# A two-layer hybrid decoder trunk: the third and the last right factor of each seven-product block summed by accumulating loads

## The chip, the cores and the metric

The kernel runs on one core of one Trainium2 chip. The metric is the device time of one execution in microseconds. The engines are called PE (TensorE: matmuls and their weight loads), DVE (VectorE), ACT (ScalarE), POOL (GpSimd) and SP (SyncE, which here issues loads). DRAM-to-SBUF loads run on 16 DMA engines that all issuing queues share.

## The reference

256 tokens of width 1024 go through two layers, each of an FFN, a mixer (a state-space part, pooling and attention) and a second FFN, with norms around each. The change touches the FFNs alone:

```python
def _swiglu(h, wg, wu, wd):
    return (jax.nn.silu(h @ wg) * (h @ wu)) @ wd

for l in range(DEPTH):                      # DEPTH = 2
    f = _swiglu(_rmsnorm(h, ff1_norm_pre[l]), ff1_w_gate[l], ff1_w_up[l], ff1_w_down[l])
    h = h + 0.5 * _rmsnorm(f, ff1_norm_post[l])
    ...                                     # the mixer
    f = _swiglu(_rmsnorm(h, ff2_norm_pre[l]), ff2_w_gate[l], ff2_w_up[l], ff2_w_down[l])
    h = h + 0.5 * _rmsnorm(f, ff2_norm_post[l])
```

`wg` and `wu` are 1024 x 2816, `wd` is 2816 x 1024, all float32.

## The kernel before, in words

**Precision.** A weight of 1 MB (128 partitions x 2048 floats, 8 KB each) is loaded into a place called `raw`. It is then split into a rounded part `hi` (a copy on ACT, line 98) and the rest `lo` (raw minus hi, on DVE, line 99), each in two steps of 128x1024. Activations are split in the same way (lines 199 and 200). Every product is then three passes of matmuls: hi by hi, hi by lo, lo by hi.

**The FFN.** The 2816 columns are 11 units of 256. Units 0 and 1 are done plainly (`ffn_first`); 4, 7 and 10 as pairs of a gate and an up product (`ffn_pair`, lines 285 to 287); 2 and 3, 5 and 6, 8 and 9 as blocks of seven products in place of eight (`ffn_quad`, line 416). For a block let g1, g2 be the upper and lower half (512 rows) of its gate columns and u1, u2 those of its up columns. The right factors are

| name | value | before |
|---|---|---|
| g1, g2, u2 | as loaded | as loaded |
| T1 | g1 + u1 | DVE add, into u1's place |
| T2 | T1 + u2 | DVE add, into u1's place |
| T3 | u1 + u2 = T2 - g1 | DVE subtraction, into g1's place |
| T4 | T2 + g2 | DVE add, into u1's place |

Each add or subtraction stands on line 97, in two steps of 128x1024, ahead of the split of its sum. There are 12 blocks (three in each of four FFNs), so 48 sums and 96 steps. The left factors are sums of quarters of the activations, made once per FFN (S1 to S4). Behind each block or pair the down projections of the units before it follow (`mm_rows`, line 322): the hidden activations are turned by PE (line 391), copied and split by ACT and DVE (199, 200) into buffers of the tag "t", and multiplied with two token tiles in turn. In the first two blocks of an FFN a down projection stands between two of the products; in the last (units 8 and 9, `late`) none stands before u2's.

**What sets the order.** `plan_ffn` lists loads (`W.unit`) and splits (`W.job`). There are four places for raw weights and five for split ones; `pump` loads as soon as a place is free and splits as soon as fewer than five splits are held. A place is given back when the last job that reads it has been split (`free`). `product` and `mm_rows` take splits in the order in which PE is to use them. The framework then orders the instructions of each engine once, when the program is built; on the chip each engine takes its queue strictly in order, and one that waits holds all that is behind it. Loads are issued by SP; POOL has only the 28 reciprocal square roots of the norms (line 210) and five settings of constants at the start.

In the places below, `hiN` and `loN` are the splits of the N-th job, `rawN` is the place of the N-th load, `t` and `wk` are temporaries in SBUF and PSUM.

Of the kernel before, what the change touches and what calls it, by code (L numbers as in the profile page):

```python
# [13 lines left out]
AF = mybir.ActivationFunctionType  # L14
ALU = mybir.AluOpType
AX = mybir.AxisListType

P = 128
# [10 lines left out]
UNIT = 2048  # L29
# [18 lines left out]
class Weights:  # L48
# [9 lines left out]
        self.units.append((src, cols))  # L58
        return len(self.units) - 1

    def job(self, unit, sum_of=None, free=(), pieces=2):


        self.jobs.append((unit, sum_of, free, pieces))
        return len(self.jobs) - 1

    def plan(self, src, cols=UNIT, pieces=2):
# [17 lines left out]

    def split_next(self):
        i, nc = self.split, self.nc
        u, sum_of, free, pieces = self.jobs[i]
        cols, raw = self.units[u][1], self.raw[u]
        hi = self.splitp.tile([P, KD * QDT], F32R, tag="hi", name=f"hi{i}")  # L90
        lo = self.splitp.tile([P, KD * QDT], F32R, tag="lo", name=f"lo{i}")
        step = cols // pieces
        for c in range(0, cols, step):
            s = slice(c, c + step)
            if sum_of:
                x, op, y = sum_of
                nc.vector.tensor_tensor(raw[:, s], self.raw[x][:, s], self.raw[y][:, s], op=op)  # L97
            nc.scalar.activation(hi[:, s], raw[:, s], AF.Copy)  # L98
            nc.vector.tensor_tensor(lo[:, s], raw[:, s], hi[:, s].bitcast(F32), op=ALU.subtract)  # L99
        for v in free:  # L100
            del self.raw[v]
            self.live -= 1
        self.parts[i] = (hi, lo)
        self.split += 1
        self.held += 1
# [25 lines left out]
def hybrid_trunk_kernel(ctx: ExitStack, tc: tile.TileContext, a, out: bass.AP):  # L131
    nc = tc.nc
# [3 lines left out]
    tmp = ctx.enter_context(tc.tile_pool(name="tmp", bufs=1))  # L136
# [3 lines left out]
    ids = iter(range(10**6))  # L140

    def buf(dtype=F32, n=512, tag="t"):
        return tmp.tile([P, n], dtype, tag=tag, name=f"{tag}{next(ids)}", bufs={"t": 22, "n": 8}[tag])

    def tiny(n):
        return small.tile([P, n], F32, tag=f"s{n}", name=f"s{next(ids)}", bufs=2 if n > 64 else 12)
# [1 line left out]
    def bank(tag="wk"):  # L148
        return psum.tile([P, 512], F32, tag=tag, name=f"{tag}{next(ids)}")
# [176 lines left out]
    def plan_ffn(l, n):  # L326


        p = {}

        def down(i):
            p["d", i] = W.plan(a[f"ff{n}_d"][l, i])

        def pair(i):
            for k in "gu":
                p[k, i] = W.plan(a[f"ff{n}_{k}"][l, PAIRS.index(i)])

        for i in range(2):
            for k in range(2):
                p["f", i, k] = W.plan(a[f"ff{n}_f"][l, 2 * i + k], pieces=4)  # L340
        before = list(FIRST)
        for i in range(2, NU):
            if i in PAIRS:
                pair(i)
                for b in before:
                    down(b)
                before = [i]
            elif i in QUADS:
                src = a[f"ff{n}_q"][l, QUADS.index(i)]
                g1, u1, u2 = (W.unit(src[k]) for k in (0, 1, 3))  # L350
                p["T1", i] = W.job(u1, (g1, ALU.add, u1))
                p["g1", i] = W.job(g1)
                p["T2", i] = W.job(u1, (u1, ALU.add, u2))
                p["T3", i] = W.job(g1, (u1, ALU.subtract, g1), free=(g1,))
                late = i == QUADS[-1]
                if not late:
                    down(before[0])
                g2 = W.unit(src[2])
                p["g2", i] = W.job(g2)
                for b in before[1:]:  # L360
                    down(b)
                p["T4", i] = W.job(u1, (u1, ALU.add, g2), free=(u1, g2))
                p["u2", i] = W.job(u2, free=(u2,))
                if late:
                    down(before[0])
                before = [i, i + 1]
        for b in before:
            down(b)
        return p
# [40 lines left out]
    def product(ps, left, job, first):  # L410

        hi, lo = (w[:, :UNIT].rearrange("p (k n) -> p k n", k=4) for w in W.get(job))
        parts = [(k, i) for k in range(4) for i in range(2)] + [(k, 2) for k in range(4)]
        for n, (k, i) in enumerate(parts):
            x, w = ((left[0], hi), (left[0], lo), (left[1], hi))[i]
            nc.tensor.matmul(ps, x[:, k, :], w[:, k, :], start=first and n == 0, stop=n == len(parts) - 1,  # L416
                             skip_group_check=not first)
        W.done(job)

    def ffn_quad(i, p, left, turn, downs):  # L420


        late = i == QUADS[-1]
        turn(0)
        pc = bank()
        product(pc, left["S1"], p["T1", i], True)
        h1 = buf()
        nc.scalar.activation(h1, pc, AF.Copy)
        pa = bank()
        product(pa, left["X11"], p["g1", i], True)  # L430
        w2 = buf()
        nc.scalar.activation(w2, pa, AF.Copy)
        turn(1)
        W.pump()
        pb = bank()
# [1 line left out]
        nc.vector.tensor_tensor(w2, pb, w2, op=ALU.add)  # L437
        nc.vector.tensor_tensor(pc, pc, w2, op=ALU.subtract)  # L438
        W.pump()
        pd = bank()  # L440
        product(pd, left["S3"], p["T3", i], True)
        nc.vector.tensor_tensor(pd, pd, w2, op=ALU.add)
        nc.vector.tensor_tensor(h1, h1, pd, op=ALU.subtract)
        W.pump()
        if not late:
            downs[0]()
        product(pa, left["X12"], p["g2", i], False)
        h0 = buf()
        nc.scalar.activation(h0, pa, AF.Silu)
# [609 lines left out]
```

## Time and profile before

| | |
|---|---|
| runs | median 964.05 us of 3 (962.85 to 965.3) |
| profiled execution | 964.58 us, of which the span is 962.5 us |
| PE, DVE, ACT busy | 940.0, 814.6, 584.3 us |
| line 97 (sums of factors) | 96 steps, 113.7 us on DVE |
| line 99 (lo), 128x1024 | 344 steps, 403.6 us on DVE |
| loaded | 176 MB; DMA engines 49.6% of their time |
| PE's granted clock | 0.991 on average |

Busy times are unions of an engine's instructions. Matmuls are pipelined and their ends are modelled, so their rate is read from the starts of consecutive ones: 12 matmuls with 512 columns take 2.72 us undisturbed. A place where PE loses time shows as more time between two such starts, and only partly as idle time. In a timeline, a number in brackets is the engine's idle time before the row and what ended it.

### The profile page before, as it was taken

How to read it: one execution, taken by the hardware profiler on the slowest of the kernel's cores; microseconds unless marked ns; L12 is line 12 of the kernel's file. 1: busy time of each engine (PE TensorE's matmuls, PEld its weight loads, DVE VectorE, ACT ScalarE, POOL GpSimd, SP SyncE). 2: the span in 40 equal slices, each digit the busy share in tenths (PEclk: the TensorE clock that was granted, in tenths of full speed). 3: DMA queues.
4: the chain of work that ended last, by engine and by line, in shares of the span. 5: the costliest groups of instructions: out<-in, count | busy, mean ns of one | idle time of the engine just before them, and what ended most of it. 6: DMA issues, size and time to landing. Idle time of an engine off the chain costs nothing.

```text
span 962.5 us, 13043 instructions
## 1 busy us (share of the span) xinstructions
PE 940.0 (98%) x5064; PEld 800.9 (83%) x5064; DVE 814.6 (85%) x1088; ACT 584.3 (61%) x923; POOL 19.7 (2%) x33
## 2 busy tenths in 40 slices
PE   8999999999999999999999999999999999999997
PEld 5679898988988779898977888898888877979895
DVE  5997899688797989899598989986878798889982
ACT  7665566467656565566466656666584565656651
POOL 0000000010001000000000000000000100000000
PEclk9989999999999999999999999999999999999999
DMA  7464365755243355466642727293733242927241
GB/s 295 186 251 186 144 250 206 277 182 212 88 144 116 109 210 228 158 236 232 249 175 81 295 109 284 95 362 135 268 124 131 88 154 88 345 92 300 93 177 44
DMA packets 26706, 178.03 MB, mean 185 GB/s; under 512 B 2962, under 2 KB 3346, under 8 KB 6292
## 3 DMA queue, kind: packets, MB, share of 16 engines
q1 hardware_dynamic: 26644, 177.19, 49.6%
q8 instruction: 40, 0.66, 0.3%
q14 instruction: 22, 0.18, 0.1%
HBM read 176.13 MB, written 1.05 MB: 184 GB/s over the span
## 4 chain that ended last, share of the span: by engine, by line
PE 77%; DVE 13%; ACT 5%; issue 2%; DMA 2%; POOL 1%; SPq 0%; DVEq 0%; POOLq 0%; ACTq 0%
PE acc L322 25%; PE wk L416 21%; PE wk L286 6%; PE wk L285 6%; PE wk L287 6%; DVE lo L99 6%; PE wk L307 5%; DVE raw L97 3%; ACT hi L98 2%; ACT n L216 1%; PE wk L391 1%; DMA raw<-in_ff_q 1%; DVE n L200 1%; POOL s L210 1%; PE wk L852 1%
## 5 line engine op out<-in xcount | busy, mean ns | idle before, releaser
L98 ACT ACTIVATE hi<-raw 128x1024 fp32r<-128x1024 f32 (+2 forms) x440 | 399.3, 958 | 179.6 <-DVE raw L97 57.6
L99 DVE TENSOR_TENSOR lo<-raw,hi 128x1024 fp32r<-128x1024 f32 (+2 forms) x440 | 466.1, 1100 | 15.7 <-ACT hi L98 14.7
L322 PE MATMUL acc<-hi,t 128*128 128x512 f32 x832 | 238.4, 395 | 3.3 <-DVE t L200 1.4
L322 PEld LDWEIGHTS acc<-hi,t 128*128 128x128 f32 x832 | 154.4, 188 | 38.5 <-ACT t L199 4.5
L285 PE MATMUL wk<-xT,hi 128*128 128x256 f32 x544 | 156.1, 287 | 0.0
L286 PE MATMUL wk<-xT,hi 128*128 128x256 f32 x544 | 154.8, 285 | 0.0
L287 PE MATMUL wk<-xT,lo 128*128 128x256 f32 x544 | 154.7, 284 | 0.0
L322 PE MATMUL acc<-lo,t 128*128 128x512 f32 x416 | 133.0, 391 | 4.1 <-DVE lo L99 4.1
L307 PE MATMUL wk<-hi,xT 128*128 128x512 f32 x384 | 124.4, 399 | 3.8 <-ACT xT L199 2.2
L416 PE MATMUL wk<-hi,n 128*128 128x512 f32 x384 | 126.6, 394 | 0.0
L97 DVE TENSOR_TENSOR raw<-raw,raw 128x1024 f32<-128x1024 f32 x96 | 113.7, 1216 | 2.5 <-DMA raw<-in_ff_q 2.5
L286 PEld LDWEIGHTS wk<-xT,hi 128*128 128x128 f32 x544 | 105.1, 193 | 0.7
L285 PEld LDWEIGHTS wk<-xT,hi 128*128 128x128 f32 x544 | 105.1, 193 | 0.6
L287 PEld LDWEIGHTS wk<-xT,lo 128*128 128x128 f32 x544 | 104.9, 193 | 0.1
L322 PEld LDWEIGHTS acc<-lo,t 128*128 128x128 f32 x416 | 77.7, 188 | 21.9 <-DVE lo L99 5.9
L416 PE MATMUL wk<-hi,xT 128*128 128x512 f32 x288 | 94.6, 389 | 0.0
L307 PEld LDWEIGHTS wk<-hi,xT 128*128 128x128 f32 x384 | 72.9, 191 | 21.4 <-ACT xT L199 3.3
L416 PEld LDWEIGHTS wk<-hi,n 128*128 128x128 f32 x384 | 73.1, 190 | 15.7 <-DVE wk L438 0.2
L307 PE MATMUL wk<-lo,xT 128*128 128x512 f32 x192 | 76.2, 398 | 0.6 <-DVE lo L99 0.6
L416 PE MATMUL wk<-lo,n 128*128 128x512 f32 x192 | 75.8, 395 | 0.0
L416 PEld LDWEIGHTS wk<-hi,xT 128*128 128x128 f32 x288 | 54.1, 188 | 11.6
L199 ACT ACTIVATE t<-wk 128x256 fp32r<-128x256 f32 x72 | 26.9, 378 | 54.7 <-PE wk L391 34.6
(182 smaller groups left out, 840.1 us busy)
## 6 DMA issues: line engine op xcount, KB each, us to landing
raw<-in_ff_q SPq DMA_DIRECT2D x48, 1024.0 KB, 7.1
raw<-in_ff_d SPq DMA_DIRECT2D x44, 1024.0 KB, 7.0
raw<-in_ff_f SPq DMA_DIRECT2D x15, 1024.0 KB, 5.1
raw<-in_ff_g SPq DMA_DIRECT2D x12, 1024.0 KB, 5.3
raw<-in_ff_u SPq DMA_DIRECT2D x12, 1024.0 KB, 4.9
raw<-in_w_in SPq DMA_DIRECT2D x10, 1024.0 KB, 5.6
raw<-in_w_kvz SPq DMA_DIRECT2D x8, 1024.0 KB, 7.0
raw<-in_w_out SPq DMA_DIRECT2D x8, 1024.0 KB, 4.9
```

Source lines behind the costliest of these rows:

```text
L97: nc.vector.tensor_tensor(raw[:, s], self.raw[x][:, s], self.raw[y][:, s], op=op)
L98: nc.scalar.activation(hi[:, s], raw[:, s], AF.Copy)
L99: nc.vector.tensor_tensor(lo[:, s], raw[:, s], hi[:, s].bitcast(F32), op=ALU.subtract)
L199: nc.scalar.activation(hi, src_f32, AF.Copy)
L200: nc.vector.tensor_tensor(lo, src_f32, hi.bitcast(F32), op=ALU.subtract)
L210: nc.gpsimd.tensor_tensor(r, v, halfexp, op=ALU.pow)
L285: nc.tensor.matmul(ps, hi[:, k, s], x[0][:, k, :], start=k == 0, stop=False)
L286: nc.tensor.matmul(ps, hi[:, k, s], x[1][:, k, :], start=False, stop=False)
L287: nc.tensor.matmul(ps, lo[:, k, s], x[0][:, k, :], start=False, stop=k == KD - 1)
L307: nc.tensor.matmul(ps, y[:, k, :], w[:, k, :], start=h == 0 and n == 0, stop=h == 1 and n == len(parts) - 1)
L322: nc.tensor.matmul(acc[b], x[:, j, s], w[:, j, b * 512 : (b + 1) * 512], start=first and j == 0 and i == 0, stop=last and j == 1 and i == 2)
L416: nc.tensor.matmul(ps, x[:, k, :], w[:, k, :], start=first and n == 0, stop=n == len(parts) - 1, skip_group_check=not first)
```

## The change

The block's sums are made differently. T1 is summed by DVE into g1's place (after g1 itself has been split), T2 too. u2 is loaded a second time, onto u1 in u1's place, by a load that adds to what is there: this makes T3. g2 is loaded a second time onto T2 in g1's place: this makes T4. Both loads are issued by POOL, T3's when T1 has been summed and u1 is read no more, T4's when T2 has been split. The first product is g1's, then T1's; T3's split comes after the next down projection's, and that down projection ahead of T3's product (not in the last block). The temporaries of tag "t" are 20 instead of 22, and the space for descriptors of POOL's loads is 4096 instead of 1024 bytes.

```diff
-    def job(self, unit, sum_of=None, free=(), pieces=2):
-        self.jobs.append((unit, sum_of, free, pieces))
+    def job(self, unit, sum_of=None, free=(), pieces=2, then=None):
+        self.jobs.append((unit, sum_of, free, pieces, then))
...
             nc.scalar.activation(hi[:, s], raw[:, s], AF.Copy)
             nc.vector.tensor_tensor(lo[:, s], raw[:, s], hi[:, s].bitcast(F32), op=ALU.subtract)
+        if then:
+            nc.gpsimd.dma_start(self.raw[then[0]][:, :UNIT], then[1], accum_op=ALU.add)
...
-        return tmp.tile([P, n], dtype, tag=tag, name=f"{tag}{next(ids)}", bufs={"t": 22, "n": 8}[tag])
+        return tmp.tile([P, n], dtype, tag=tag, name=f"{tag}{next(ids)}", bufs={"t": 20, "n": 8}[tag])
...
                 g1, u1, u2 = (W.unit(src[k]) for k in (0, 1, 3))
-                p["T1", i] = W.job(u1, (g1, ALU.add, u1))
                 p["g1", i] = W.job(g1)
-                p["T2", i] = W.job(u1, (u1, ALU.add, u2))
-                p["T3", i] = W.job(g1, (u1, ALU.subtract, g1), free=(g1,))
+                p["T1", i] = W.job(g1, (g1, ALU.add, u1), then=(u1, src[3]))
+                p["T2", i] = W.job(g1, (g1, ALU.add, u2), then=(g1, src[2]))
                 late = i == QUADS[-1]
                 if not late:
                     down(before[0])
+                p["T3", i] = W.job(u1, free=(u1,))
                 g2 = W.unit(src[2])
-                p["g2", i] = W.job(g2)
+                p["g2", i] = W.job(g2, free=(g2,))
                 for b in before[1:]:
                     down(b)
-                p["T4", i] = W.job(u1, (u1, ALU.add, g2), free=(u1, g2))
+                p["T4", i] = W.job(g1, free=(g1,))
                 p["u2", i] = W.job(u2, free=(u2,))
...
         turn(0)
+        pa = bank()
+        product(pa, left["X11"], p["g1", i], True)
+        w2 = buf()
+        nc.scalar.activation(w2, pa, AF.Copy)
         pc = bank()
         product(pc, left["S1"], p["T1", i], True)
         h1 = buf()
         nc.scalar.activation(h1, pc, AF.Copy)
-        pa = bank()
-        product(pa, left["X11"], p["g1", i], True)
-        w2 = buf()
-        nc.scalar.activation(w2, pa, AF.Copy)
         turn(1)
...
+        if not late:
+            downs[0]()
         pd = bank()
         product(pd, left["S3"], p["T3", i], True)
         nc.vector.tensor_tensor(pd, pd, w2, op=ALU.add)
         nc.vector.tensor_tensor(h1, h1, pd, op=ALU.subtract)
         W.pump()
-        if not late:
-            downs[0]()
         product(pa, left["X12"], p["g2", i], False)
...
-    nc = _bacc.Bacc("TRN2", target_bir_lowering=False, num_devices=1, dynamic_dma_scratch_size=1024)
+    nc = _bacc.Bacc("TRN2", target_bir_lowering=False, num_devices=1, dynamic_dma_scratch_size=4096)
```

The lines shift: 97 becomes 98 (sums), 98 becomes 99 (hi), 99 becomes 100 (lo), 199 and 200 become 202 and 203, 322 becomes 325, 375 becomes 378, 391 becomes 394, 416 becomes 419, 210 becomes 213; the accumulating load is line 102.

**First place: DVE, the first FFN's first block.** `raw4` is g1, `raw5` u1, `raw6` u2, `raw7` the next down projection. Before:

```order
L97 TENSOR_TENSOR raw5_223<-raw4_211,raw5_223 128x1024 x2
L375 TENSOR_TENSOR t41_309<-wk39_258,t40_307 128x512
L99 TENSOR_TENSOR lo4_250<-raw5_223,hi4_249 128x1024
L99 TENSOR_TENSOR lo5_366<-raw4_211,hi5_365 128x1024
L99 TENSOR_TENSOR lo4_250<-raw5_223,hi4_249 128x1024
L99 TENSOR_TENSOR lo5_366<-raw4_211,hi5_365 128x1024
L375 TENSOR_TENSOR t45_363<-wk43_312,t44_361 128x512
L97 TENSOR_TENSOR raw5_223<-raw5_223,raw6_235 128x1024 x2
L97 TENSOR_TENSOR raw4_211<-raw5_223,raw4_211 128x1024
L99 TENSOR_TENSOR lo6_372<-raw5_223,hi6_371 128x1024 x2
L99 TENSOR_TENSOR lo7_380<-raw4_211,hi7_379 128x1024
L97 TENSOR_TENSOR raw4_211<-raw5_223,raw4_211 128x1024
```

And with the change:

```order
L100 TENSOR_TENSOR lo4_250<-raw4_211,hi4_249 128x1024 x2
L378 TENSOR_TENSOR t41_307<-wk39_256,t40_305 128x512
L98 TENSOR_TENSOR raw4_211<-raw4_211,raw5_223 128x1024 x2
L100 TENSOR_TENSOR lo5_364<-raw4_211,hi5_363 128x1024 x2
L378 TENSOR_TENSOR t45_361<-wk43_310,t44_359 128x512
L98 TENSOR_TENSOR raw4_211<-raw4_211,raw6_235 128x1024 x2
L203 TENSOR_TENSOR t47_398<-wk50_401,t46_397 128x2x128
L100 TENSOR_TENSOR lo6_373<-raw4_211,hi6_372 128x1024
L100 TENSOR_TENSOR lo7_382<-raw7_247,hi7_381 128x1024
L100 TENSOR_TENSOR lo6_373<-raw4_211,hi6_372 128x1024
L100 TENSOR_TENSOR lo7_382<-raw7_247,hi7_381 128x1024
L100 TENSOR_TENSOR lo8_390<-raw5_223,hi8_389 128x1024 x2
```

g1's split now stands first and T1's sum behind it; T3's two steps on `raw4` are gone, the down projection's split (`raw7`) stands ahead of T3's (`lo8` from `raw5`), which was ahead of it.

**Second place: ACT, the second FFN's first block.** `hi62` is T2 (before), `hi63` T3 and `hi64` the down projection before; with the change `hi62` is T2, `hi63` the down projection and `hi64` T3. `t331` and `t333` are the hi parts of the turned hidden activations of units 0 and 1; `wk335` holds the first token tile's, `wk340` the second's. Before:

```order
L199 ACTIVATE t331_3085<-wk335_3089 128x2x128
L98 ACTIVATE hi63_3067<-raw51_2620 128x1024
L98 ACTIVATE hi64_3077<-raw54_2898 128x1024
L98 ACTIVATE hi63_3067<-raw51_2620 128x1024
L98 ACTIVATE hi64_3077<-raw54_2898 128x1024
L199 ACTIVATE t333_3087<-wk335_3089 128x2x128
L199 ACTIVATE t331_3085<-wk340_3128 128x2x128
```

And with the change:

```order
L99 ACTIVATE hi62_3054<-raw51_2614 128x1024
L99 ACTIVATE hi63_3063<-raw54_2892 128x1024
L99 ACTIVATE hi62_3054<-raw51_2614 128x1024
L99 ACTIVATE hi63_3063<-raw54_2892 128x1024
L99 ACTIVATE hi64_3071<-raw52_2868 128x1024 x2
L202 ACTIVATE t331_3079<-wk335_3083 128x2x128
L202 ACTIVATE t331_3079<-wk340_3122 128x2x128
L202 ACTIVATE t333_3081<-wk335_3083 128x2x128
```

The first tile's turn stood ahead of T3's hi; now both tiles' turns stand behind T3's, which comes from the place that the accumulating load fills. In the first FFN's first block the first tile's turn is still ahead of T3's hi, and the second tile's is behind it.

**Third place: DVE, the first FFN's last block**, with the change (`raw23` is g1, `raw24` u1, `raw25` u2, `raw26` g2):

```order
L98 TENSOR_TENSOR raw23_957<-raw23_957,raw25_1002 128x1024 x2
L378 TENSOR_TENSOR t91_1167<-wk87_1050,t90_1165 128x512
L100 TENSOR_TENSOR lo31_1183<-raw23_957,hi31_1182 128x1024
L203 TENSOR_TENSOR t83_1046<-wk89_1156,t82_1045 128x2x128
L203 TENSOR_TENSOR t93_1170<-t91_1167,t92_1169 128x512
L203 TENSOR_TENSOR t85_1048<-wk89_1156,t84_1047 128x2x128
L100 TENSOR_TENSOR lo31_1183<-raw23_957,hi31_1182 128x1024
L100 TENSOR_TENSOR lo32_1216<-raw24_980,hi32_1215 128x1024 x2
L100 TENSOR_TENSOR lo33_1248<-raw26_1024,hi33_1247 128x1024 x2
L100 TENSOR_TENSOR lo34_1286<-raw23_957,hi34_1285 128x1024 x2
```

Between T2's split (`lo31`) and T4's (`lo34`, from the place that the second accumulating load fills) only T3's and g2's splits stand; no sum is left behind T2's. On PE this block's order is g1, T1, T2, T3, g2, nine matmuls of u2, T4.

More of the change, by code (lines that the diff above doesn't have):

```diff
@@ L87, in split_next @@
         i, nc = self.split, self.nc
-        u, sum_of, free, pieces = self.jobs[i]
+        u, sum_of, free, pieces, then = self.jobs[i]
         cols, raw = self.units[u][1], self.raw[u]
```

## The prediction

> **What bounds the kernel now.** I read the page's first part, then a table of stretches of 20 us, then, where TensorE (PE) loses time, the timelines of PE, VectorE (DVE) and ScalarE (ACT) and the chain of waits.
>
> ```profile
> span 962.5 us, 13043 instructions
> PE 940.0 (98%) x5064; PEld 800.9 (83%) x5064; DVE 814.6 (85%) x1088; ACT 584.3 (61%) x923; POOL 19.7 (2%) x33
> ```
>
> ```profile
> 40.00:60.00 20.00, 16.46 (x59) 12.19 (x58) 17.82 (x21) 12.14 (x16) 0.00 (x0) 0.83 0.29 108
> ...
> 320.00:340.00 20.00, 18.67 (x84) 14.54 (x82) 20.00 (x25) 12.21 (x18) 0.00 (x0) 1.00 0.11 44
> ...
> 360.00:380.00 20.00, 20.00 (x139) 18.68 (x138) 18.43 (x21) 12.96 (x17) 0.00 (x0) 1.00 0.76 293
> ...
> 500.00:520.00 20.00, 18.83 (x88) 15.13 (x87) 19.90 (x25) 11.87 (x17) 0.00 (x0) 1.00 0.09 34
> ...
> 800.00:820.00 20.00, 18.81 (x84) 14.97 (x83) 17.47 (x20) 11.52 (x15) 0.00 (x0) 1.00 0.34 114
> 820.00:840.00 20.00, 20.00 (x127) 18.10 (x127) 17.45 (x20) 12.47 (x16) 0.00 (x0) 1.00 0.98 374
> ```
>
> The columns are busy us (instructions) of PE, its weight loads, DVE, ACT and POOL, then PE's clock, the DMA share and GB/s. PE is the bound: 98% busy, and full in a stretch such as 360 to 380 however hard DVE works beside it. What is open lies at the first block of three-factor sums in each of the four FFNs (about 40, 330, 515 and 805 us). The first is by far the largest:
>
> ```profile
> 44.93 0.73 PE L322 MATMUL acc<-hi,t 128*128 128x512 f32 x2
> 46.15 0.73 PE L322 MATMUL acc<-hi,t 128*128 128x512 f32 x2 [0.48 <-ACT t L199]
> 48.51 1.21 PE L322 MATMUL acc<-lo,t 128*128 128x512 f32 x4 [1.63 <-DVE lo L99]
> 51.12 2.07 PE L322 MATMUL acc<-hi,t 128*128 128x512 f32 x4 [1.39 <-DVE t L200]
> 52.99 0.63 PE L416 MATMUL wk<-hi,n 128*128 128x512 f32 x1
> ```
>
> ```profile
> 53.19 7.41 PE wk L416 x24
> 60.60 2.72 PE acc L322 x12
> 63.32 2.72 PE wk L416 x12
> ...
> 71.48 5.44 PE wk L416 x24
> ...
> 148.28 13.60 PE wk L416 x60
> ...
> 830.49 9.17 DMA raw<-in_ff_q
> ```
>
> In the chain of waits (start, us, what) 12 matmuls take 2.72 us. The 12 of the first down projection run from 44.93 to 52.99, 8.06 us: 5.3 lost. The next 24 take 7.41 where 24 take 5.44 later, in the stretch whose clock is 0.83: 2.0 more. So 7.3 us are lost here, and PE waited each time for DVE or for ACT behind DVE. DVE has no gap there:
>
> ```profile
> 31.29 2.35 DVE L97 TENSOR_TENSOR raw<-raw,raw 128x1024 f32<-128x1024 f32 x2
> 33.56 0.68 DVE L375 TENSOR_TENSOR t<-wk,t 128x512 f32<-128x512 f32 x1
> 34.16 4.62 DVE L99 TENSOR_TENSOR lo<-raw,hi 128x1024 fp32r<-128x1024 f32 x4
> 38.70 0.68 DVE L375 TENSOR_TENSOR t<-wk,t 128x512 f32<-128x512 f32 x1
> 39.30 3.48 DVE L97 TENSOR_TENSOR raw<-raw,raw 128x1024 f32<-128x1024 f32 x3
> 42.70 3.49 DVE L99 TENSOR_TENSOR lo<-raw,hi 128x1024 fp32r<-128x1024 f32 x3
> 46.11 1.22 DVE L97 TENSOR_TENSOR raw<-raw,raw 128x1024 f32<-128x1024 f32 x1
> 47.24 3.49 DVE L99 TENSOR_TENSOR lo<-raw,hi 128x1024 fp32r<-128x1024 f32 x3
> 50.65 0.75 DVE L200 TENSOR_TENSOR t<-wk,t 128x256 fp32r<-128x256 f32 x2
> ```
>
> **The change part by part.** *Removed:* of the 96 adds below, 48.
>
> ```profile
> L97 DVE TENSOR_TENSOR raw<-raw,raw 128x1024 f32<-128x1024 f32 x96 | 113.7, 1216 | 2.5 <-DMA raw<-in_ff_q 2.5
> L210 POOL TENSOR_TENSOR s<-s,halfexp 128x1 f32<-128x1 f32 x28 | 19.4, 694 | 937.7 <-ACT s L208 780.5 <-DVE s L205 157.2
> ```
>
> Back to back one step of such an add or a split is 1.14 us (2.27 a pair, by the starts above), so DVE loses some 55 us of work. Nearly all of it lies under a full PE and is worth nothing there; it counts only in the four first blocks.
>
> *Added:* 24 loads of 1 MB that add to what is there, issued by POOL. No row of before shows one. The nearest:
>
> ```profile
> raw<-in_ff_q SPq DMA_DIRECT2D x1, 1024.0 KB, 4.8
> ```
>
> ```profile
> raw<-in_ff_q SPq DMA_DIRECT2D x48, 1024.0 KB, 7.1
> ```
>
> The first is one of them nearly alone (issued at 523.0), the second the median. 1 MB at the 374 GB/s of the fullest stretch is 2.8 us, so some 2.0 of the 4.8 are fixed. If an accumulating load moves its bytes twice (source and what is there), it takes 2.0 + 5.6 = 7.6, and with 0.7 for POOL to take it up (a POOL operation, above) 8.3 us alone. Lower bound: no dearer than a plain one, 4.8. Upper bound: twice the slowest plain landing of the chain, 2 x 9.17 = 18.3. I take 9.7, that is 8.3 and half of another megabyte beside it, since after each first sum (a first block's DMA is nearly empty: 0.11 in 320 to 340) it has little company. I call it L, from DVE's last add to the landing.
>
> The Trainium skill has the same doubling, in "Collectives: The Full Stack", section "The bandwidth ceiling: the fold count and why AG ≠ RS ≠ AR": an add in the DMA path halves the rate since both sources go through one read ring. With "DMA: Bandwidth & Descriptors", section "Anatomy of one DMA — SWDGE (gpsimd) path" (2.0 us and bytes by 436 GB/s) that would be an estimate of 6.8 us; the sum would then come out 2 us better than below. No run here shows either yet.
>
> *First block of the first FFN.*
>
> ```profile
> 336.50 3.90 ACT L98 ACTIVATE hi<-raw 128x1024 fp32r<-128x1024 f32 x4 [3.69 <-DVE raw L97]
> ```
>
> A hi on ACT is 1.06 us, and 0.95 back to back (four in 3.90 here). New order on DVE from 31.3: g1's two lo (33.6), an L375 (34.2), T1's adds (36.5), T1's lo (38.8), L375 (39.4), T2's adds (41.6), a turn's lo (42.0), lo of T2 and of the down projection in turn (46.5). The two T3 adds that stood ahead of the down projection's lo are gone, and T3's own lo stands behind it. The load into T3's place starts at 36.5 and lands at 36.5 + L = 46.2. ACT comes to T3's hi at about 44.5 (four hi of 0.95 behind T2's first add), so it waits 1.7; T3's two hi end at 48.2, and behind them in ACT's queue stand the second turn's copies, which the down projection's second half needs: 49.0. PE: g1 and T1 as T1 and g1 before, 38.75 to 44.2, turn 44.7, first half of the down projection held by the lo at 46.5 to 47.9, wait of 1.1 to 49.0, 4 matmuls (49.9), T2 (52.6), 8 matmuls (54.4), T3 (57.1). Before, the product that follows the same work starts at 63.3 at the latest (chain). **Gain 6.0 us**, by the rule 7.1 - (L - 8.6); the clock does not sag either if the wait stays near 1.
>
> *First blocks of the others.*
>
> ```profile
> 316.62 2.35 DVE L97 TENSOR_TENSOR raw<-raw,raw 128x1024 f32<-128x1024 f32 x2
> ...
> 335.25 2.35 DVE L97 TENSOR_TENSOR raw<-raw,raw 128x1024 f32<-128x1024 f32 x2
> ...
> 337.86 4.62 DVE L99 TENSOR_TENSOR lo<-raw,hi 128x1024 fp32r<-128x1024 f32 x4
> ```
>
> ```profile
> 338.56 0.73 PE L322 MATMUL acc<-hi,t 128*128 128x512 f32 x2 [0.23 <-ACT hi L98]
> 340.26 0.73 PE L322 MATMUL acc<-lo,t 128*128 128x512 f32 x2 [0.97 <-DVE lo L99]
> ...
> 343.13 0.39 PE L416 MATMUL wk<-hi,n 128*128 128x512 f32 x1
> ```
>
> Here 14 matmuls take 4.57 us for 3.18: 1.4 lost. T3's adds (335.25) go, so the down projection's lo are ready at about 337.4. But in the new order T3's hi and lo stand ahead of both turns' (second place of the order shown ahead), and the turn's lo comes only after T3's two lo, at 340.3. PE, there at 338.1, does four matmuls and waits till 340.3: 1.4 again, from a start 0.4 sooner. The load starts at 320.1 (T1's adds end 1.1 later than at 318.97, behind one of g1's lo) and ACT comes to T3 at 334.1: hidden up to L = 14. **Gain 0.4** here and at 805; at 515 the same count gives 0.1.
>
> *Later blocks.* PE is full there. What could hurt is a load that lands late, above all in each FFN's last block, where six products follow without a down projection:
>
> ```profile
> 132.78 2.35 DVE L97 TENSOR_TENSOR raw<-raw,raw 128x1024 f32<-128x1024 f32 x2
> ```
>
> New order: g1's lo in the gap from 130.7, T1's adds to 135.3, then T1's lo, T2's adds and T2's lo with the turns between, to 144.7. T3 is multiplied third of the five products from 148.28, at 156.4, so its load has until 154.1: L up to 18.8. T4's place is free at 144.7; T4 follows T3, g2 and 9 matmuls of u2, at 163.8, its split must begin by 161.5: L up to 16.8. With L of 9.7 to 12.5 (8.3 and one megabyte and a half beside it) both are covered: cost 0. DVE's queue stands while it waits for a load, but it has lost 4.6 us of adds per block.
>
> *POOL's queue:* behind a waiting accumulating load stand only later ones; the square roots (L210) come a stage later. *SP's queue:* T3's place is given back only after the landing and T3's split, but the next load that is needed, g2, takes the down projection's place, whose split now ends at 46.5, ahead of T3's. *Two buffers fewer (22 to 20):* the mixers' order on DVE and PE is unchanged; 0 taken, up to 2 if a copy waits there. *g1 ahead of T1:* the first product needs one load and no add; taken in above.
>
> **Sum:** 6.0 + 0.4 + 0.1 + 0.4 = 6.9. The profiled execution took 964.58 (span 962.5 and 2.1 around it), half a microsecond above the runs' median of 964.05: 957.7 of 964.58, or some **957.5 us**. A change under 0.3%, 2.9 us, can't be told from none.
>
> **Rivals.**
> 1. *Slower: the accumulating loads land late.* ACT and DVE take the queue in order, so a late landing holds the turns and lo behind T3. Beyond 14 us three more first blocks pay 1 us per us, beyond 16.8 four last blocks too. At L = 14 the gain is still 1.7 + 0.9 = 2.6; with four blocks paying it is gone at **14.7**, the point from which this decides. At 16, 5.4 slower (970); at 18.3 2.6 + 12.0 + 6.0 = 20.6 slower (985). For it: nothing in before bounds the operation itself, and 820 to 840 shows the DMA at 0.98 just after a first block, when T4's load is under way. Against: T3's load, which decides first, runs in an emptier stretch.
> 2. *No change: the wait moves.* With L near 13 the first block keeps 7.1 - 4.4 = 2.7 and the others 0.9, less a microsecond of the buffers or the clock: 961 to 963. The second half of the down projection behind T3 in ACT's queue speaks for it.
>  The Trainium skill's "SBUF — State Buffer", section "Who interferes with whom", has a mechanism for this: POOL can be locked out from writing descriptors while DVE holds a shared port. By our rows that would be up to four DVE operations back to back, 4.62 us, L of 12.9 and 962 us. The same section excepts TENSOR_TENSOR by inference, and nearly all of DVE's work here is that; I leave it 5 in 100 of this rival.
> 3. *More gain.* With L at 4.8 to 8 the first block gives its 7.3, the other first blocks all their waits (1.4, 1.2 by the table at 800, 1.2 at 515): 11 us, 953.
> 4. *The change doesn't remove work:* if T3 and T4 still had adds, L97 would stay at x96; the new order shows them gone, so under 1 in 100.
>
> **How the numbers follow.** Forecast 0.53, rival 1 0.22, rival 2 0.17, rival 3 0.08. Faster: 0.53 + 0.08, less a little for a forecast that ends under 2.9: 0.60; same: rival 2 and that little, 0.18; slower 0.22. The range takes in rival 3 at its best (the 11 us and 2 of noise, 951) and rival 1 up to L = 16 (970), leaving out its tail: 951 to 971; the forecast's own is 954 to 961.
>
> **What would show it.** Right: L97 at x48 and some 57 us; PE's matmuls of the first down projection ending near 54 and the third factor's near 57; the clock at 1.00 in 40 to 60; the accumulating loads landing in 8 to 12 us; 360 to 380 still full. Wrong: PE waiting at the last blocks (about 160, 450, 630, 915) for ACT's hi behind an accumulating load; landings over 14; PE idle at 340 and 805 grown.

## The result, and the profile after

The changed kernel takes **977.31 us** (median of 6 runs, 973.62 to 978.76) beside 964.67 of the kernel before (6 runs): a ratio of 1.0122, with a 95% interval of 1.0093 to 1.0151. It is slower by 1.2%; 957.5 was forecast, and 971 as the end of the range. The profiled execution has a span of 977.0 us for 962.5 before.

From the page of the changed kernel: the first part, the sums, and POOL's loads with their median time from issue to landing.

```profile
span 977.0 us, 13173 instructions
PE 947.7 (97%) x5064; PEld 801.2 (82%) x5064; DVE 763.6 (78%) x1040; ACT 579.9 (59%) x923; POOL 43.0 (4%) x57
...
L98 DVE TENSOR_TENSOR raw<-raw,raw 128x1024 f32<-128x1024 f32 x48 | 56.9, 1220 | 0.0
...
raw<-in_ff_q POOLq DMA_DIRECT2D x24, 1024.0 KB, 8.0
```

The change does what it says. Half of the sums are gone and DVE is busy for 51 us less. An accumulating load lands in 8.0 us in the median. So these parts were forecast well, and the whole went the other way.

Both kernels run 5064 matmuls, so the start of the n-th in one trace can be set beside that of the n-th in the other. This table, worked out from both traces, shows where the difference arises:

| matmul | place | before, us | after, us | after minus before |
|---|---|---|---|---|
| 217th | first FFN, first block, at its last products | 66.8 | 62.6 | -4.2 |
| 289th | behind that block | 80.1 | 79.8 | -0.3 |
| 1801st | second FFN, first block, ahead of T4 | 355.4 | 355.0 | -0.4 |
| 1873rd | behind that block | 368.3 | 371.0 | +2.7 |
| 2665th | third FFN, first block | 517.6 | 520.3 | +2.8 |
| 2809th | behind it | 548.5 | 555.9 | +7.4 |
| 3673rd | a mixer | 699.6 | 707.8 | +8.3 |
| 3745th | 72 matmuls later | 710.8 | 722.0 | +11.2 |
| 4321st | fourth FFN, first block | 819.6 | 830.4 | +10.8 |
| 4393rd | behind T4 there | 833.4 | 847.6 | +14.3 |

The gain of the first FFN was there (4.2 us) and was lost again within 20 us. The first blocks of the other three lost 3.1, 4.6 and 3.5. The 2.9 us near 715 belong to the clock: it was granted at 0.88 in 700 to 720, with no wait of PE there. Other kernels below show the same step at that place or don't, with and without the change's parts; each was traced once, and the mean clock of the executions of one and the same kernel differs by as much (0.992 to 0.997 in the last kernel of run 9). Of the losses in the first and the third FFN, too, some 1.7 us each are clock: it stood at 0.5 for 3.4 us there, just behind a wait of PE (the 0.91 in the stretches below).

In the table of stretches of the changed kernel (busy us and count of PE, its weight loads, DVE, ACT, POOL; clock, DMA share, GB/s), DVE now has gaps just where PE loses time:

```profile
40.00:60.00 20.00, 18.36 (x78) 13.46 (x77) 13.39 (x17) 10.95 (x15) 0.88 (x1) 1.00 0.80 209
60.00:80.00 20.00, 18.07 (x86) 15.05 (x86) 19.57 (x20) 15.44 (x17) 0.00 (x0) 0.91 0.94 358
...
340.00:360.00 20.00, 17.90 (x76) 13.98 (x76) 13.26 (x17) 12.54 (x16) 0.00 (x0) 1.00 0.77 272
...
540.00:560.00 20.00, 17.78 (x98) 15.36 (x97) 19.90 (x20) 12.25 (x14) 0.00 (x0) 0.91 0.95 364
...
700.00:720.00 20.00, 20.00 (x130) 16.93 (x129) 16.70 (x44) 12.92 (x35) 0.00 (x0) 0.88 0.52 186
```

The second FFN's first block shows how. The rows below are of the timelines of POOL, SP, ACT, DVE and PE there, one engine under the other: start, us, what; in brackets the idle time ahead and what ended it.

```profile
336.21 0.86 POOL L102 DMA_DIRECT2D raw<-in_ff_q  x1 [14.08 <-DVE lo L100]
...
338.20 0.33 SPq L78 DMA_DIRECT2D raw<-in_ff_q  x1
...
347.57 2.01 ACT L99 ACTIVATE hi<-raw 128x1024 fp32r<-128x1024 f32 x2 [5.12 <-DMA raw<-in_ff_q]
...
342.49 0.42 DVE L203 TENSOR_TENSOR t<-wk,t 128x256 fp32r<-128x256 f32 x1 [0.83 <-ACT t L202]
348.67 2.36 DVE L100 TENSOR_TENSOR lo<-raw,hi 128x1024 fp32r<-128x1024 f32 x2 [5.75 <-ACT hi L99]
350.94 0.69 DVE L440 TENSOR_TENSOR t<-wk,t 128x512 f32<-128x512 f32 x1
...
352.27 6.89 DVE L100 TENSOR_TENSOR lo<-raw,hi 128x1024 fp32r<-128x1024 f32 x6
359.08 0.70 DVE L447 TENSOR_TENSOR wk<-wk,t 128x512 f32<-128x512 f32 x1
359.68 1.22 DVE L100 TENSOR_TENSOR lo<-raw,hi 128x1024 fp32r<-128x1024 f32 x1
360.81 0.69 DVE L448 TENSOR_TENSOR t<-t,wk 128x512 f32<-128x512 f32 x1
...
358.22 0.61 PE L325 MATMUL acc<-hi,t 128*128 128x512 f32 x2
361.64 0.47 PE L419 MATMUL wk<-hi,xT 128*128 128x512 f32 x1 [2.80 <-DVE t L448]
```

Read it from the end. At 361.64 PE starts T4's product after a wait of 2.80 us. That product adds into the PSUM bank of T3's (`pd`), so it waits for the two DVE operations that read it, L447 and L448. T3's product itself ended at about 350. L447 starts only at 359.08, since in DVE's queue it stands behind eight `lo`, and the first of these waited 5.75 us for ACT's `hi` of g2, and that for g2's load. This is the plain load that SP issued at 338.20, two microseconds after POOL had issued T4's accumulating load (336.21). While DVE stood from 342.9 to 348.7, L440 was behind g2's `lo` too, although the product that it reads, T2's, had ended at about 344.6.

Before, the same two readers (there L442 and L443) ended at 358.77 and PE started T4 at 359.02, without a wait: there was a quarter of a microsecond of slack, which no view of waits shows. DVE's second reader and PE's first matmul of T4, from the kernel before:

```profile
358.09 0.68 DVE L443 TENSOR_TENSOR t<-t,wk 128x512 f32<-128x512 f32 x1
...
359.02 0.39 PE L416 MATMUL wk<-hi,xT 128*128 128x512 f32 x1
```

What the DMA engines did meanwhile shows in short stretches of the changed kernel:

```profile
338.00:342.00 4.00, 2.98 (x13) 2.03 (x13) 3.54 (x6) 1.57 (x4) 0.00 (x0) 1.00 0.95 186
342.00:344.00 2.00, 2.00 (x11) 1.62 (x10) 0.42 (x1) 0.45 (x2) 0.00 (x0) 1.00 0.90 266
344.00:348.00 4.00, 4.00 (x19) 3.33 (x18) 0.00 (x0) 0.43 (x1) 0.00 (x0) 1.00 1.01 422
```

Under the accumulating load the DMA engines are 0.95 busy and move 186 GB/s; when it is through, nearly full too, 422. The view of the DMA queues for 338 to 342 has POOL's queue (q0: packets, MB, share of the engines) and none of SP's:

```profile
q0 software_dynamic: 91, 0.75, 95.2%
```

In the trace the first packet of g2's load starts at 342.43, 4.2 us after its issue; that of the lone load of before that was issued at 523.02 starts after 0.97. In the chain of waits of the whole run g2's load appears in each FFN's first block; that of before has no g2 (its load at 830.49 is one for the next block):

```profile
46.73 9.63 DMA raw<-in_ff_q
338.20 9.29 DMA raw<-in_ff_q
523.95 8.31 DMA raw<-in_ff_q
815.62 9.43 DMA raw<-in_ff_q
```

And PE's waits, by who ended them (us in total, times, longest), have a new first line and a new third. Both are T4's product: in the fourth FFN an ACT operation ended at the same moment as L448 and got the name.

```profile
PE wk L419 <- DVE t L448: 7.0, 3, 2.8
PE acc L325 <- DVE t L203: 3.1, 3, 1.1
PE wk L419 <- ACT hi L99: 2.8, 1, 2.8
```

### The profile page after: what moved, and what is told of

The parts are those of the page before. It is cut to its first block, busy times and chain, and to the rows that moved or that the text cites. A ratio compares the mean times of both kernels' runs of the same rounds, so it can differ in the third digit from the quotient of the medians.

```text
span 977.0 us, 13173 instructions
## 1 busy us (share of the span) xinstructions
PE 947.7 (97%) x5064; PEld 801.2 (82%) x5064; DVE 763.6 (78%) x1040; ACT 579.9 (59%) x923; POOL 43.0 (4%) x57
## 4 chain that ended last, share of the span: by engine, by line
PE 64%; DVE 17%; ACT 6%; issue 5%; DMA 5%; POOL 1%; SPq 0%; POOLq 0%; DVEq 0%; ACTq 0%
PE acc L325 19%; PE wk L419 16%; DVE lo L100 10%; PE wk L289 6%; PE wk L288 6%; PE wk L290 6%; PE wk L310 5%; DMA raw<-in_ff_q 5%; ACT hi L99 3%; DVE raw L98 2%; ACT n L219 1%; POOL s L213 1%; PE wk L394 1%; DVE n L203 1%; DMA raw<-in_ff_f 1%
## 5 line engine op out<-in xcount | busy, mean ns | idle before, releaser
L310 PE MATMUL wk<-hi,xT 128*128 128x512 f32 x384 | 123.8, 397 | 2.9 <-ACT xT L202 2.6
L419 PE MATMUL wk<-hi,xT 128*128 128x512 f32 x288 | 97.9, 401 | 10.0 <-DVE t L448 7.0
L310 PE MATMUL wk<-lo,xT 128*128 128x512 f32 x192 | 76.4, 399 | 0.6 <-DVE lo L100 0.6
L419 PE MATMUL wk<-lo,xT 128*128 128x512 f32 x144 | 57.8, 402 | 0.8 <-DVE lo L100 0.8
L98 DVE TENSOR_TENSOR raw<-raw,raw 128x1024 f32<-128x1024 f32 x48 | 56.9, 1220 | 0.0
```

What stands on the lines that cost most here:

```text
L310: nc.tensor.matmul(ps, y[:, k, :], w[:, k, :], start=h == 0 and n == 0, stop=h == 1 and n == len(parts) - 1)
```

## The experiments

**Theory A**: T4's accumulating load holds the DMA engines for six microseconds just ahead of g2's load; DVE's queue stands for g2; what stands behind comes late, T3's readers above all, and T4's product pays. **Rival B**: the moved down projection alone took the slack between T3's product and T4's. **Rival C**: the two buffers fewer or the descriptor space.

**1. The order alone.** Everything as changed, but T3 and T4 summed by DVE:

```diff
-p["T1", i] = W.job(g1, (g1, ALU.add, u1), then=(u1, src[3]))
+p["T1", i] = W.job(g1, (g1, ALU.add, u1))
-p["T3", i] = W.job(u1, free=(u1,))
+p["T3", i] = W.job(u1, (u1, ALU.add, u2), free=(u1,))
 (T2 and T4 likewise: T4 = W.job(g1, (g1, ALU.add, g2), free=(g1, g2)))
```

> The changed kernel's order of products, splits and down projections, its 20 buffers and its descriptor space, but T3 and T4 summed by VectorE again: no accumulating load is left. Theory A (the accumulating load for T4 takes the DMA engines while g2's load waits behind it, VectorE's queue stands for g2's split, and the two operations on T3's bank that stand behind it come late, so that T4's product, which goes into that bank, waits 2.1 to 3.0 us in the first block of each FFN): these four waits go, the old losses of the first FFN's first block come back, 963 to 968 us. Rival B (the moved down projection alone takes the slack between T3's product and T4's): the four waits stay at 2 us or more and the old losses come back on top, 973 to 982. Rival C (the two buffers fewer or the descriptor space): 973 to 979, with the loss at other places.

967.25 us, ratio 1.0035 (1.0019 to 1.0050). No wait for L448 is left in the list of PE's waits. The moved down projection alone is not what costs 12 us, so B falls.

**2. The same loads, not adding.** The kernel leaves out the sums T3 and T4; all else stays.

```diff
-nc.gpsimd.dma_start(self.raw[then[0]][:, :UNIT], then[1], accum_op=ALU.add)
+nc.gpsimd.dma_start(self.raw[then[0]][:, :UNIT], then[1])
```

> The changed kernel with its 24 loads by POOL left in place but no longer adding: they overwrite, so T3 and T4 are just u2 and g2 and these sums are left out. Order, waits and the number of loads stay; only the operation in the DMA differs. Theory A: a load that doesn't add lands in some 5 us instead of 8.4 and leaves the DMA engines 2.9 us sooner, g2's load lands 2 to 3 us sooner, and most of the four waits at T4's product goes: 966 to 970. Rival B (order alone): waits as they are, 975 to 979. Rival C: 975 to 979.

965.06 us, ratio 1.0009 (0.9993 to 1.0024). POOL's loads land in 5.1 us instead of 8.0, and T4's four waits, 1.9, 2.8, 2.2 and 2.8 us in the changed kernel, fall to 1.2, 1.0, 0.5 and 1.4. Of this kernel, POOL's loads, PE's waits for T3's readers, and the stretch that answers to 338 to 342 above:

```profile
raw<-in_ff_q POOLq DMA_DIRECT2D x24, 1024.0 KB, 5.1
```

```profile
PE wk L419 <- DVE t L448: 2.6, 3, 1.2
```

```profile
334.00:338.00 4.00, 2.95 (x14) 1.99 (x13) 3.42 (x6) 1.55 (x5) 0.00 (x0) 1.00 0.94 385
```

Same order, same number of loads, same share of the DMA engines; only 385 GB/s for 186. The 12.2 us between this kernel and the changed one are the price of adding in the loads, T3's and T4's together.

**3. More work ahead of T4's product.** u2's product goes first, in the plan (the two jobs change places, not shown) and on PE:

```diff
-product(pd, left["X22"], p["T4", i], False)   (with its SiLU and product)
 product(pc, left["S4"], p["u2", i], False)
 nc.vector.tensor_tensor(h0, pc, h0, op=ALU.mult)
+product(pd, left["X22"], p["T4", i], False)
```

> The changed kernel with the product of u2 (which goes into another bank) ahead of T4's: 2.72 us of matmuls stand between. Theories A and B both say that the wait is at T3's bank: 2.1 + 3.0 + 2.4 + 3.0 = 10.5 us of waits in the profile are covered but for 0.3 each, 966 to 968 us. Rival C, or a wait that only moves on to u2's split: 974 to 978.

975.85 us, ratio 1.013 (1.010 to 1.016): 8 us above what both theories gave. The wait for L448 is gone, but in the second, third and fourth FFN PE now waits 2.4, 2.7 and 2.4 us further on, in the down projection behind the next pair, for the copies of the turned activations in ACT's queue. The fourth wait of this line, 1.5 us, lies inside the first FFN's first block; that FFN waits 1.1 us for DVE further on:

```profile
PE acc L325 <- ACT t L202: 9.0, 4, 2.7
```

DVE still stands for g2 (6.24 us in the second FFN), and ACT's copies stand behind `hi` that wait for DVE's sums. T4's bank was only the first place where the delay came out. This sharpened theory A: what is lost is DVE's time, not a slot of PE's.

**4 and 5. One of the two loads alone.** In the first T3 is accumulated and T4 is DVE's; in the second the other way round.

```diff
-p["T2", i] = W.job(g1, (g1, ALU.add, u2), then=(g1, src[2]))
+p["T2", i] = W.job(g1, (g1, ALU.add, u2))
-p["g2", i] = W.job(g2, free=(g2,))
+p["g2", i] = W.job(g2)
-p["T4", i] = W.job(g1, free=(g1,))
+p["T4", i] = W.job(g1, (g1, ALU.add, g2), free=(g1, g2))
```

> The changed kernel with only T3 summed by an accumulating load; T4 is an add of VectorE in g1's place again, with g2 as it is loaded once. Theory A: nothing holds g2's load any more, the four waits at T4's product fall under 0.5 us each although VectorE has 27 us more to do, and the 4.2 us that the first FFN's first block had gained stay: 959 to 965. Rival B: waits stay at 2 to 4 us, 974 to 980. Rival C: 973 to 979.

> The mirror of the last run: T4 by an accumulating load, T3 by two adds of VectorE (u1 plus u2 in u1's place). Theory A: T4's load still stands ahead of g2's at the DMA engines, so the waits of the four first blocks come back (2 to 3 us each, at T4's product or, where VectorE is late, in the block behind it), and the first FFN's first block loses its T3 gain too: 970 to 978 us. Rival (T3's load, or the two together, make the loss): 960 to 967.

959.78 us for T3 alone, ratio 0.9958 (0.9943 to 0.9973): faster than before. 988.41 for T4 alone, ratio 1.0258 (1.021 to 1.031): slower than the whole change, and by more than theory A gave. With runs 1 and the result the four make a square (us):

| | T4 by DVE | T4 by an accumulating load |
|---|---|---|
| T3 by DVE | 967.25 | 988.41 |
| T3 by an accumulating load | 959.78 | 977.31 |

T3's load is worth 7 to 11 us, T4's costs 17 to 21. The change is the sum of a good half and a bad one. With T3 alone no wait of PE for L448 is left, and DVE's timeline shows g2 come in time: its first reader there, T4's add, waits 0.17 us, at the place where the changed kernel's DVE stood for 5.75.

```profile
337.49 0.42 DVE L203 TENSOR_TENSOR t<-wk,t 128x256 fp32r<-128x256 f32 x1 [0.83 <-ACT t L202]
338.08 1.23 DVE L98 TENSOR_TENSOR raw<-raw,raw 128x1024 f32<-128x1024 f32 x1 [0.17 <-DMA raw<-in_ff_q]
```

In the kernel with T4 alone the chain of waits has g2's load with 10.74 us:

```profile
339.49 10.74 DMA raw<-in_ff_q
```

**6. Buffers and descriptor space**, put into the kernel before:

```diff
-bufs={"t": 22, "n": 8}[tag]  ...  dynamic_dma_scratch_size=1024
+bufs={"t": 20, "n": 8}[tag]  ...  dynamic_dma_scratch_size=4096
```

> The kernel before with 20 instead of 22 buffers of the tag t and 4096 bytes of descriptor space, nothing else. Theory A: no part of the loss, 962 to 966 us. Rival C: 967 or more; the 2.9 us that all kernels with 20 buffers so far lose near 715 us, where the granted clock was 0.50 in the changed kernel, would be the buffers' and show here too.

965.01 us, ratio 1.0004 (0.9985 to 1.0023); the step near 715 us is not there. C falls.

**7. T4's load behind g2's.** It reads g2 where SP's load has put it, so it can't start before g2 has landed:

```diff
-p["T2", i] = W.job(g1, (g1, ALU.add, u2), then=(g1, src[2]))
-p["g2", i] = W.job(g2, free=(g2,))
+p["T2", i] = W.job(g1, (g1, ALU.add, u2))
+p["g2", i] = W.job(g2, then=(g1, g2), free=(g2,))
 (the load's source is then the place of g2)
```

> The changed kernel, but T4's accumulating load reads g2 from its place on the chip, as SyncE has loaded it, and so starts only after g2's load has landed; nothing stands ahead of g2's load any more, and both adds stay off VectorE. Theory A: the stand of VectorE's queue for g2 goes (5.7 us near 345 in the changed kernel, 2 or less here), and with it the waits, unless T4 itself lands too late: g2 at about 344, T4 at 352 to 353, its split at 355 to 356, needed at 358: 958 to 965 us. Rival B (order): 974 to 979. Rival (an accumulating load costs wherever it stands): 970 to 980.

1003.87 us, ratio 1.040 (1.035 to 1.044): 39 us above theory A's range and 24 above the last rival's. At the disputed place it does what A says (DVE stands 1.16 us for g2 near 350, not 5.75). But T4 itself now lands too late, in the second block of each FFN above all. The list of PE's waits of this kernel, and the row of ACT's timeline in one such block, where the queue stands 8.92 us for T4's load:

```profile
PE wk L420 <- DVE t L449: 24.4, 8, 5.0
```

```profile
410.52 7.69 ACT L99 ACTIVATE hi<-raw 128x1024 fp32r<-128x1024 f32 x8 [8.92 <-DMA raw<-raw]
```

The same jam with another load at its head: T4's `hi` stands ahead of ACT's and DVE's later work, T3's readers among it. That load was issued at 398.98 and took 11.5 us: a plain load that SP issued 0.1 us later went first. Its own first packet starts 5.0 us after its issue; in the first blocks of this kernel that is 1.4.

**8. Mending the kernel with T3 alone.** Its profile has four waits left in the first blocks (0.94, 1.17, 1.21, 1.23 us by the starts of the matmuls, 0.8 to 1.1 of idle time), for the turned activations, which stand behind T3's `hi` and `lo` in the queues. T3's split is held back there:

```diff
+                if i == QUADS[0]:
+                    W.hold.add(p["T3", i])
...
         turn(1)
+        W.hold.discard(p["T3", i])
         W.pump()
...
-            elif self.split < len(self.jobs) and self.held < SPLIT_BUFS and self.ready():
+            elif self.split not in self.hold and self.split < len(self.jobs) and self.held < SPLIT_BUFS and self.ready():
```

> The kernel with only T3 accumulated, and T3's split in each FFN's first block held back until both turns of the hidden activations are emitted, so that T3's hi and lo no longer stand ahead of the turns in the queues of ScalarE and VectorE. If these two splits are what the turns wait for, the waits of 0.94, 1.17, 1.21 and 1.23 us (profile of the kernel with T3 alone, at 47.9, 334, 516 and 804 us) go: 955 to 957.5. If T3's product then waits instead, 959 to 961.

**956.12 us, ratio 0.9919 (0.9891 to 0.9947)**: faster than both kernels. The four waits are gone; in the last three FFNs waits of 0.5 to 0.6 us at the next product have come in their place. PE is full in the stretches where the first two FFNs lost time:

```profile
40.00:60.00 20.00, 20.00 (x92) 16.54 (x91) 19.15 (x23) 13.64 (x18) 0.00 (x0) 1.00 0.69 191
340.00:360.00 20.00, 20.00 (x101) 16.84 (x100) 19.26 (x20) 14.81 (x16) 0.00 (x0) 1.00 0.75 290
```

**9. Fewer accumulating loads.** The same kernel with T3's load only in each FFN's first block (4 of 12), and with none at all, T3's add being held back together with its split:

```diff
-p["T1", i] = W.job(g1, (g1, ALU.add, u1), then=(u1, src[3]))
+p["T1", i] = W.job(g1, (g1, ALU.add, u1), then=(u1, src[3]) if i == QUADS[0] else None)   (none: no then)
-p["T3", i] = W.job(u1, free=(u1,))
+p["T3", i] = W.job(u1, None if i == QUADS[0] else (u1, ALU.add, u2), free=(u1,))   (none: always the add)
```

> The kernel with T3 accumulated and its split held back, but the accumulating load only in the first block of each FFN (4 loads instead of 12); in the other eight T3 is an add of VectorE in u1's place. If the later blocks cost and gain nothing, as predicted there, the time is that of the kernel it is taken from: 954.5 to 957.5 us. If the loads disturb others in the later blocks, 952 to 954; if VectorE's 18 us of adds there were worth something, 959 to 963.

> No accumulating load at all: the changed order with VectorE's adds, and T3's add and split in each FFN's first block held back until both turns are emitted. If the gain of the T3 kernel is one of order alone, 955 to 958 us. If VectorE's two steps of T3's add must go to win it (they now stand ahead of T3's product instead of ahead of the turns, 2.3 us in each first block), T3's product waits and the time is 960 to 966.

957.38 us, ratio 0.9918 (0.9889 to 0.9948), and 956.81, ratio 0.9922 (0.9900 to 0.9944). The three can't be told apart: their intervals leave some 3 us open. Within that, the later blocks indeed gain nothing from T3's load, and the first blocks don't need it either. With the new order, nearly all that had to go from ahead of the turns was T3's work; it need not go off DVE. A remainder may be worth its load: in the one trace of each, the 289th matmul starts 6.7, 6.1 and 4.9 us sooner than before in the kernels with 12, 4 and no loads. The kernel with no accumulating load still has all its sums on DVE:

```profile
L99 DVE TENSOR_TENSOR raw<-raw,raw 128x1024 f32<-128x1024 f32 x96 | 114.6, 1216 | 11.0 <-DMA raw<-in_ff_q 10.9
```

**10. Is T4's load harmless in the other blocks?** The kernel of 8 with T4 accumulated in the eight blocks that aren't the first of their FFN:

```diff
-p["T2", i] = W.job(g1, (g1, ALU.add, u2))
+p["T2", i] = W.job(g1, (g1, ALU.add, u2), then=None if i == QUADS[0] else (g1, src[2]))
 (g2's place freed and T4's job as in the change, for those blocks)
```

> The kernel with T3 accumulated and its split held back, and T4 accumulated too, as the change has it, but only in the eight blocks that are not the first of their FFN. Theory A: all of the change's loss is in the first blocks, where g2's load is issued 2 us behind T4's and VectorE has no work to go on with: 954.5 to 958 us. If T4's loads cost in the other blocks too (0.3 to 0.6 us a block is what the changed kernel lost in second blocks), 958 to 962; if the collision is general, 965 or more.

965.26 us, ratio 1.0017 (1.0002 to 1.0033), 9.1 more than without. So T4's loads are not harmless in the other blocks, and theory A's forecast for them is wrong. In the changed kernel itself the second blocks lost only 0.6 or less. Here T4's product waits there for 1.8, 1.6, 1.5 and 2.5 us, in the same way, and the chain of waits has g2's load again. PE's waits in all, and that load in the first two FFNs:

```profile
PE wk L422 <- DVE t L452: 7.8, 5, 2.5
```

```profile
92.96 8.53 DMA raw<-in_ff_q
381.46 8.61 DMA raw<-in_ff_q
```

T4's load is issued at 90.96 here, 2 us ahead of g2's, as in the first blocks of the changed kernel. In the changed kernel's second block the two are 3.3 us apart (94.75 and 98.05) and g2 lands in 7.0.

## Why the prediction was wrong

**L was right.** 8.3 alone and 9.7 with company were forecast, from DVE's last add to the landing. T3's first load took 9.3 (36.6 to 45.9). The view of line 102 has the landings from POOL's issue, some 0.6 us behind that add, and who waited for one of the 24 (us, times):

```profile
who waited for it (us, times):
  ACT hi L99: 1.3, 1
...
DMA to landing us min/median/max: 7.7/8.0/9.9
```

One wait of 1.3 us in all: ACT's for T3 in the first FFN, where 1.7 was forecast. By this view nothing else in the run waits for an accumulating load, and it is still these loads that cost the time.

**The first block of the first FFN was right up to T3.** T1's adds end at 36.6 (36.5 forecast) and the load into T3's place lands at 45.9 (46.2). T3's product ends at 57.3 where 57.1 was forecast, and the clock is 1.00 in 40 to 60. PE's rows there, T3's last four matmuls and g2's first:

```profile
56.36 1.07 PE L419 MATMUL wk<-hi,n 128*128 128x512 f32 x4
57.55 0.51 PE L419 MATMUL wk<-hi,xT 128*128 128x512 f32 x1
58.81 0.50 PE L419 MATMUL wk<-lo,xT 128*128 128x512 f32 x1 [0.75 <-DVE lo L100]
```

Of the 6.0 us of gain, 5.9 existed at that moment (T3's last matmul, the 200th, starts at 62.93 before and at 57.04 here). Then g2 was late (0.75 us, above), T4's product waited 1.9, and the clock, at 0.91 in 60 to 80, took some 1.9 more: in the chain of waits 22 matmuls take 6.89 us, at 12 in 2.72 they would take 5.0.

```profile
69.69 6.89 PE wk L419 x22
```
The sum stopped one product too early.

**The step that failed** is the paragraph on queues: "the next load that is needed, g2, takes the down projection's place". It looked at when g2's load can be *issued* and took no term for its landing. It did not ask which load would be in the DMA engines then. The answer was in the text: T4's place is free when T2's `lo` are done, and the down projection's place soon after, so T4's load had to be issued just ahead of g2's in every first block. By the prediction's own numbers (T4's load through 8.3 us after its issue, 2.8 us for g2's megabyte behind it, g2 issued 2 us later, 4.8 for a lone landing) g2 would land some 4 us late; in the four first blocks it landed in 9.6, 9.3, 8.3 and 9.4. Runs 4 and 5, against the result and run 1, show T4's accumulating load at 17 to 21 us over the whole kernel, and run 2 shows 12 of the change's time to be the adding itself; the term was taken as 0.

**T4 was checked for the wrong thing.** "L up to 16.8" covers T4's own landing, and T4 did land in time: nothing waited for it (above). What T4's product waited for was T3's bank. The moved down projection had stood between T3's product and T4's; without it and with DVE late, two small operations behind eight splits decide. The prediction never named `pd`.

**Rival 1 had the sign and the wrong variable.** It let the time turn at a landing of 14.7 us of the accumulating loads themselves. They landed in 8.0, and the time rose by 12.6. Its one sentence in favour, the DMA at 0.98 just after a first block with T4's load under way, pointed at the right place. Rivals 2 and 3 needed an L that did not occur.

**Later blocks at cost 0**: T3's, yes (run 9); T4's, no (run 10). Why the changed kernel itself loses next to nothing there is not shown; its two loads are further apart (3.3 us for 2.0). **Two buffers fewer at 0**: right (run 6). **Other first blocks, gain 0.4, 0.1, 0.4**: the wait for the turn stayed, at 1.0 to 1.1 us where 1.4 was forecast, and run 8 shows that the reason given for it, T3's split ahead of the turns, was the right one.

**What the removal of the adds was worth.** The prediction ascribed the 6 us to adds that leave DVE. Run 9 shows that most of it comes from T3's work being moved behind the turns: 4.9 us at the 289th matmul with every sum on DVE.

**A slip in the working.** For a landing of 6.8 us the text gives a sum 2 us better, while its rival 3 gives 11 us for landings of 4.8 to 8, which is 4 better. With landings near 8 neither came to matter.

What stays open: whether T4's load costs more when T3 is summed by DVE (by the medians 21 for 17 us; the four executions of run 5 spread over 7 us, and by the two pairs of traced executions it is 16 for 18), and when the clock steps down. It did behind T4's waits of 1.9 and 2.2 us and did not behind those of 2.8, and near 715 us it did without any.

## What to carry to other kernels

A load that is moved or added is priced not by its own landing alone, but by the next plain load that is issued within its time: look up which one it is, and what stands in the queues behind the split of that one. On an engine that takes its queue in order and has little slack, a wait of 5 us for a load is work lost, as it was here; covering the place where it first comes out moves the wait on to the next. Before work is taken off a busy engine, try moving it behind what the bound engine waits for: here that gave as much, to within the 3 us that the runs can tell, without a single extra byte loaded.

## What the runs showed of the hardware that was not expected

**Adding in a load costs about the same from either memory.** Run 7's loads read g2 on the chip, not in HBM, and land in 7.6 us in the median; those from HBM take 8.0, a plain one by POOL 5.1. From run 7, POOL's two kinds:

```profile
raw<-in_ff_q POOLq DMA_DIRECT2D x12, 1024.0 KB, 8.0
raw<-raw POOLq DMA_DIRECT2D x12, 1024.0 KB, 7.6
```

So reading from HBM is not what makes it slow. In the traces a packet of 8 KB takes 629 ns in the median when it adds, and 309 when it doesn't (run 2). The Trainium skill's "Collectives: The Full Stack", section "The bandwidth ceiling: the fold count and why AG ≠ RS ≠ AR", has an add in the DMA path read two sources through one ring at half the rate. The 186 GB/s against 385 of the same stretch without the add agree with that; no run here looks into the ring itself.

**An accumulating load is not a background load.** Two loads in flight did not share the engines evenly from the start. In the changed kernel's four first blocks the first packet of g2's load came 3.2, 4.2, 4.4 and 4.2 us after its issue, 0.97 for a lone load; in run 7, the other way round, an accumulating load that met a plain one waited 5.0 us for its first packet. Once both had packets, they did share: in run 5, from 343 to 348, some 130 KB a microsecond each. What holds the second load's first packet back, the traces don't show.

**POOL was not held up.** Its 24 issues take 865 ns in the median and 1025 at most, with DVE busy 78% of the time. In 23 of them the first packet starts 1.56 to 1.62 us after the issue, whether DVE was at work in that time or idle (2.37 in the first, when other loads were under way). The lockout of POOL's descriptor writes, which the Trainium skill's "SBUF — State Buffer", section "Who interferes with whom", describes, doesn't show in this kernel's TENSOR_TENSOR work, as the exception in the same section has it.
